# The first norm's sums of a hybrid decoder layer, placed later inside the first projection

## The chip, the cores and the metric

The kernel runs on one core of a Trainium2 chip. The metric is device microseconds of one execution; where several executions were timed, the median counts. The engines are named as in the profile: PE multiplies matrices (PEld loads its weights), DVE and ACT work on vectors, POOL is GpSimd, SP issues DMAs.

## The reference

One layer works on a sequence of 1024 positions and 1024 channels:

```
z = rms_norm(x, norm_mix_g);  proj = z @ w_in
u_pool, u_lru, u_gate = proj[:512], proj[512:1024], proj[1024:]
y_pool = pool_mixer(u_pool)                   # trailing windows 2, 4, 8, 16
y_lru  = rg_lru(conv(u_lru)) * gelu(u_gate)   # 4 taps, sigmoid gates, a scan
h = x + concat(y_pool, y_lru) @ w_out
h = h + square(relu(rms_norm(h) @ w_up)) @ w_down
h = h + sigmoid(rms_norm(h) @ w_gate + b) * (p @ w_proj)
out = rms_norm(h)
```

Here `rms_norm(x, g)` is `x * rsqrt(mean(x*x) + eps) * g`, with the mean over the 1024 channels of a position.

## The kernel before, in words

Channels lie on the 128 partitions and positions along the free dimension, so `x` is eight blocks `H[k]` of 128 channels by 1024 positions. Every fp32 product is made of three: an operand is split by ACT into a rounded part `hi` (L178, or L181 with the gain as a scale) and by DVE into the rest `lo` (L179, L182), and PE multiplies hi·hi, hi·lo and lo·hi (`mm`, L350). A `mm` over 1024 positions is six matmuls of 128x512.

**The first norm.** The factor rsqrt(mean) of a position isn't needed before the projection: the product is made of `x * g`, and its result is multiplied by the factor afterwards (`normed`, L535). The factor needs the sum of the squares over all channels. ACT squares each block (L386, L389), DVE adds the squares up in `T[0]` (L390); then `norm.sums()` splits that sum into hi and lo for each half of 512 positions (DVE: L414, L415; the tiles are called `hl`) and multiplies it by a matrix of ones on PE (L416, L417: four matmuls into two banks called `n_ps`, two for each half), which sums over the partitions and leaves the sum in all of them. `norm.rstd(R)` calls `sums` and goes on from the banks: DVE transposes each (L434), ACT takes the root of 16 columns for each half (L438, which first needs another activation table, ACT_TABLE_LOAD), DVE inverts it (L439) and spreads it back into `R` (L440).

**The first projection.** The three first outputs `ps_l0`, `ps_l1`, `ps_l2` (the first three blocks of `u_lru`) are built up together, since the blocks of `x` arrive one by one: for each block `k`, `mm` for `o` = 0, 1, 2, 18 matmuls in all. From `k` = 2 on that is the loop at the end of the function's part shown below. In the last block, `k` = 7, `norm.rstd(R)` is called ahead of this loop, so that its four matmuls stand on PE's queue between block 6 and block 7. The other nine outputs, `ps_i0` to `ps_i8`, follow one by one (`project`, 48 matmuls each, weights `wi0` to `wi8`).

**What follows on the other engines.** `conv(0..2)` take `ps_l0` to `ps_l2` through `normed`, a scale on ACT (L540) and three taps on DVE (L544), and split the result (`y8` to `y11` and `y20` to `y23`, hi and lo in turn). `ask_small` splits the small weights of the gates and the pool mixer, `T[5]`, into `hl` as well: ACT writes its hi (L178, `hl<-t`), DVE its lo (L179, `hl<-t,hl`). They are the same tiles `hl` that hold the hi and lo of the norm's sums, so ACT's copy can start only when the sums of the first half have been multiplied. Then come the pool windows (L621 to L631), the gates of the recurrence (`lru_gates`: `ps_g`, L571 on PE, two banks for each of two row halves; sigmoids L579 on ACT; a product L582 on DVE) and the scan (`lru_scan`: L591 to L602).

**PSUM.** Outputs take turns (`psum`): one pair of banks from `pp` (`banks`), the next two single banks from `pd` (`bank`), of which there are four. The norm's sums take two of `pd`. A name such as `ps_i4_0` is the first bank of an output in two single banks. The output `ps_g03` (gate 3, first row half) takes the two banks in which `ps_i4` was, so its matmuls wait until `normed` on DVE (L535) has read `ps_i4` out of them.

**What sets the order.** The program's layer orders the instructions of each engine by priorities that follow the order of the Python code; instructions that are "pinned" (`pin`, `keep_in_program_order`) stay where they are written. On a core each engine works its list in order; semaphores join the lists. The norm's matmuls are not pinned at this place.

Of the kernel before, what the change touches and what calls it, by code (L numbers as in the profile page):

```python
# [30 lines left out]
NT = D // P  # L31
# [27 lines left out]
def block_kernel(  # L59
# [22 lines left out]
    def fixed(name, dt):  # L82
        return pool.tile([P, S], dt, name=name)
# [27 lines left out]
    R = fixed("rstd", F32)  # L111
# [34 lines left out]
    def f32(ap):  # L146
        return ap.bitcast(F32)
# [3 lines left out]
    def turns(z):  # L151
        return z.rearrange("p (a j) -> p j a", a=2)
# [11 lines left out]
    def col(name, i):  # L164
        c = COLS[name] + i
        return vecs[:, c : c + 1]
# [3 lines left out]
    def pin(ins):  # L170
        return tc.keep_in_program_order(ins) if in_order else ins
# [3 lines left out]
    def split(src, hi, lo, g=None, eng=None):  # L175

        if g is None:
            first = pin(nc.scalar.activation(hi, src, AF.Copy))  # L178
            lowest[:] = [pin((eng or nc.vector).tensor_tensor(lo, src, f32(hi), ALU.subtract)).ins]  # L179
        else:  # L180
            first = pin(nc.scalar.activation(hi, src, AF.Identity, scale=g))  # L181
            lowest[:] = [pin(nc.vector.scalar_tensor_tensor(lo, src, g, f32(hi), ALU.mult, ALU.subtract)).ins]  # L182
        return first.ins

    def raw_tile(name):
        return wp.tile([P, S], F32, tag="raw", name=f"{name}_raw")

    def weight_tiles(name):
        return [wp.tile([P, S], F32R, tag=f"w{x}", name=f"{name}_{x}") for x in ("hi", "lo")]
# [141 lines left out]
    def ask():  # L331
        if todo:
            fn, *args = todo.pop()
            asked.append(fn(*args))

    def weights():
        ask()
        return asked.pop(0)

    def mm(parts, whi, wlo, zhi, zlo, first, last, only=None, more=False, held=False):  # L340
        outs = [
            (slice(hs.start + n, hs.start + min(n + HALF, w)), ps[:, n : min(n + HALF, w)])
            for hs, ps in parts
            for w in (hs.stop - hs.start,)
            for n in range(0, w, HALF)
            if only is None or hs.start + n == only.start
        ]
        for w, z in ((whi, zhi), (whi, zlo), (wlo, zhi)):
            for hs, ps in outs:
                ins = nc.tensor.matmul(  # L350
                    ps, w, turns(z[:, hs]),
                    start=first and z is zhi and w is whi,
                    stop=last and w is wlo,
                    skip_group_check=more,
                )
                if held:
                    tc.keep_in_program_order(ins)
                    held = False

    def kblk(t, k):  # L360
        return t[:, k * P : (k + 1) * P]
# [80 lines left out]
    def tables():  # L442

        one = ones_f[:, :16]
        tc.keep_in_program_order(
            nc.vector.tensor_tensor_scan(recip_t, one, one, 0.0, ALU.mult, ALU.add)
        )
        nc.vector.reciprocal(recip_t, recip_t)


        nc.sync.dma_start(T[5][:, FIRST], gates)
        nc.sync.dma_start(T[5][:, SECOND], pool_w)
# [5 lines left out]
    def softplus():  # L458

        c0 = COLS["lru_l"]  # L460
        lv = vecs[:, c0 : c0 + NLRU]
        with tc.issue_after(lowest[0]):
            nc.vector.tensor_scalar_mul(neg, lv, -1.0)
        nc.vector.tensor_tensor(e, lv, neg, ALU.max)
        nc.scalar.activation(e, e, AF.Exp, scale=-1.0)
        nc.vector.tensor_scalar_add(s, e, 2.0)
        nc.vector.reciprocal(s, s)
        nc.vector.tensor_tensor(s, s, e, ALU.mult)
        nc.vector.tensor_tensor(s2, s, s, ALU.mult)
        nc.vector.memset(poly, 1.0 / 19)  # L470
        for n in range(8, -1, -1):
            nc.vector.tensor_tensor(poly, poly, s2, ALU.mult)
            nc.vector.tensor_scalar_add(poly, poly, 1.0 / (2 * n + 1))
        nc.vector.tensor_tensor(poly, poly, s, ALU.mult)
        nc.vector.tensor_scalar(neg, neg, 0.0, 8.0, ALU.max, ALU.mult)
        nc.vector.scalar_tensor_tensor(cpos, poly, 16.0, neg, ALU.mult, ALU.add)
        nc.vector.tensor_scalar_mul(cneg, cpos, -1.0)

        c_b, c_s = COLS["pool_b"], COLS["pool_s"]
        with tc.issue_after(lowest[0]):  # L480
            nc.vector.tensor_tensor(pool_bs, vecs[:, c_b : c_b + NPOOL], vecs[:, c_s : c_s + NPOOL], ALU.mult)

    norm = Norm("n0", T[0], T[1:3])
# [4 lines left out]
    for k in range(NT):  # L488
        halves = HALVES if k < 2 else (slice(0, S),)
        if k == 1:  # L490
            whi, wlo = weights()
        for hs in halves:
            nc.sync.dma_start(H[k][:, hs], xT[k * P : (k + 1) * P, hs])
            if k == hs.start == 0:
                raw = raw_tile("wl0")[:, : 3 * P]
                whi, wlo = (t[:, : 3 * P] for t in weight_tiles("wl0"))
                nc.sync.dma_start(raw, w_lru[:P, :])
                pin(nc.vector.tensor_copy(whi, raw))
            split(H[k][:, hs], A[k][0][:, hs], A[k][1][:, hs], col("g_mix", k))
            if k > 1:  # L500
                whi, wlo = weights()
            if k == hs.start == 0:
                pin(nc.vector.tensor_tensor(wlo, raw, f32(whi), ALU.subtract))
        for i in AFTER[k] if k < len(AFTER) else (k,):
            norm.add(H[i])
        if k == NT - 1:
            in_order.clear()
            ask()
        if k == 2:
            softplus()  # L510
        if k == 3:
            tables()
        if k == NT - 1:
            norm.rstd(R)
        if k < 2:

            for hs in HALVES:
                for o in range(3):
                    mm(ps_l[o], kblk(whi, o), kblk(wlo, o), *A[k], k == 0, False, hs)
            continue  # L520
        for o in range(3):
            mm(ps_l[o], kblk(whi, o), kblk(wlo, o), *A[k], False, k == NT - 1)


# [157 lines left out]
    norm = Norm("n1", T[4], T[5:])  # L682
# [550 lines left out]
```

## Time and profile before

| what | value |
|---|---|
| median of 3 runs | 927.12 us |
| lowest and highest of them | 926.88 and 928.76 us |
| the profiled execution, its own time | 927.23 us |
| its span, first to last instruction | 925.4 us |
| granted TensorE clock in the span | 0.998 |
| instructions | 11180 |

The profiled execution took 1.8 us more than its span, and 0.11 us more than the median. A row of the timeline gives start and duration in us, engine, line, operation, the tile written `<-` the tiles read (without their numbers), the size and the count; in brackets stands how long the engine had been idle before it, and whose result ended that. Consecutive like instructions are merged into a row, whose duration then goes from the first start to the last end. Matmuls overlap: a 128x512 matmul shows as 0.38 us, but the next can start 0.22 us after it.

### The profile page before, as it was taken

The page shows a single profiled execution, that of the slowest core. Times are in us where ns is not written, and L with a number is a line of the kernel's source. Part 1 is how long each engine was busy: PE and PEld are TensorE (multiplying, and loading weights), DVE is VectorE, ACT ScalarE, POOL GpSimd, SP SyncE. Part 2 cuts the span into 40 slices and gives each one's busy share as a digit, 9 for nine tenths or more (in the row PEclk, how much of TensorE's full clock was granted, in tenths as well). Part 3 has the DMA queues.
Part 4 walks back from the last instruction along what each step waited for, and adds up shares of the span by engine and source line. Part 5 has one row for each costly group of instructions (what it writes and reads, how often), then busy time and mean ns, then how long its engine had stood idle before and what let it go on. Part 6 is the DMA issues. An engine that isn't in the chain of part 4 may idle for free.

```text
span 925.4 us, 11180 instructions
## 1 busy us (share of the span) xinstructions
PE 915.3 (99%) x4351; PEld 798.5 (86%) x4351; DVE 758.8 (82%) x903; ACT 456.5 (49%) x531; POOL 5.6 (1%) x7
## 2 busy tenths in 40 slices
PE   9999999999999999999999999999999999999996
PEld 7888888888888888888888888888888888888895
DVE  7997985659998888888888989979776679885676
ACT  7567893447543343344334654443444347652544
POOL 0000000002000000000000000000000000000000
PEclk9999999999999999999999999999999999999999
DMA  7210143211244345344534989366532341031022
GB/s 265 99 47 23 46 151 122 69 45 54 84 175 178 125 161 197 142 138 173 191 125 148 341 317 342 110 202 208 188 111 92 118 156 45 16 122 46 1 91 91
DMA packets 45044, 123.97 MB, mean 134 GB/s; under 512 B 4160, under 2 KB 6208, under 8 KB 44992
## 3 DMA queue, kind: packets, MB, share of 16 engines
q1 hardware_dynamic: 44848, 123.22, 38.3%
q8 instruction: 34, 0.56, 0.3%
q14 instruction: 18, 0.15, 0.0%
q10 hardware_dynamic: 144, 0.04, 0.0%
HBM read 89.69 MB, written 33.55 MB: 133 GB/s over the span
## 4 chain that ended last, share of the span: by engine, by line
PE 95%; DVE 2%; issue 1%; DMA 1%; SPq 0%; ACT 0%; DVEq 0%
PE ps_P_d L350 31%; PE ps_P_u L350 31%; PE ps_i L350 10%; PE ps_e L350 10%; PE ps_o L350 9%; PE ps_j L350 1%; DMA h<-in_xT 1%; PE ps_g L571 1%; PE ps_p L350 1%; DVE t L390 1%; PE ps_l L350 0%; DVE wl_lo L179 0%; PE n_ps L417 0%; DVE t L1093 0%; DVE a L182 0%
## 5 line engine op out<-in xcount | busy, mean ns | idle before, releaser
L350 PE MATMUL ps_P_d<-a,wd_P_hi 128*128 128x512 f32 x880 | 261.7, 379 | 0.0
L350 PEld LDWEIGHTS ps_P_d<-a,wd_P_hi 128*128 128x128 f32 x880 | 166.3, 189 | 23.6
L350 PE MATMUL ps_P_d<-a,wd_P_lo 128*128 128x512 f32 x440 | 166.8, 379 | 0.0
L350 PE MATMUL ps_P_u<-a,wu_hi 128*128 128x512 f32 x512 | 152.3, 379 | 0.0
L350 PE MATMUL ps_P_u<-y,wu_hi 128*128 128x512 f32 x384 | 114.2, 379 | 0.0
L350 PEld LDWEIGHTS ps_P_u<-a,wu_hi 128*128 128x128 f32 x512 | 96.8, 189 | 13.8
L350 PE MATMUL ps_P_u<-a,wu_lo 128*128 128x512 f32 x256 | 97.0, 379 | 0.0
L350 PEld LDWEIGHTS ps_P_d<-a,wd_P_lo 128*128 128x128 f32 x440 | 83.2, 189 | 11.8
L350 PEld LDWEIGHTS ps_P_u<-y,wu_hi 128*128 128x128 f32 x384 | 72.6, 189 | 10.4
L747 DVE TENSOR_TENSOR t<-t,ps_P_u 128x512 f32<-128x512 f32 (+1 forms) x80 | 62.6, 782 | 20.4 <-PE ps_P_u L350 20.4
L350 PE MATMUL ps_i<-a,wi_hi 128*128 128x512 f32 x288 | 74.3, 380 | 0.0
L350 PE MATMUL ps_P_u<-y,wu_lo 128*128 128x512 f32 x192 | 72.8, 379 | 0.0
L178 ACT ACTIVATE a<-wd 128x1024 fp32r<-128x1024 f32 x56 | 58.9, 1054 | 21.4 <-PE ps_P_d L350 11.6
L179 DVE TENSOR_TENSOR a<-wd,a 128x1024 fp32r<-128x1024 f32 x56 | 67.2, 1221 | 1.0 <-ACT a L178 0.6
L350 PE MATMUL ps_o<-y,wo_hi 128*128 128x512 f32 x256 | 65.7, 379 | 0.0
L350 PEld LDWEIGHTS ps_i<-a,wi_hi 128*128 128x128 f32 x288 | 54.1, 189 | 8.8 <-issue 1.0
L178 ACT ACTIVATE wu_hi<-wu 128x1024 fp32r<-128x1024 f32 x24 | 25.4, 1057 | 69.8 <-PE ps_P_u L350 44.2
L178 ACT ACTIVATE wu_hi<-wu_raw 128x1024 fp32r<-128x1024 f32 (+1 forms) x26 | 25.2, 974 | 66.3 <-PE ps_P_u L350 41.3
L350 PEld LDWEIGHTS ps_o<-y,wo_hi 128*128 128x128 f32 x256 | 48.4, 189 | 6.8
L350 PEld LDWEIGHTS ps_P_u<-a,wu_lo 128*128 128x128 f32 x256 | 48.4, 189 | 6.8
L178 ACT ACTIVATE wd_P_hi<-wd 128x1024 fp32r<-128x1024 f32 x24 | 25.3, 1054 | 46.9 <-PE ps_P_d L350 46.8
L389 ACT ACTIVATE t<-h 128x512 f32<-128x512 f32 (+2 forms) x44 | 32.0, 731 | 28.3 <-DVE h L1052 20.5
(223 smaller groups left out, 1502.8 us busy)
## 6 DMA issues: line engine op xcount, KB each, us to landing
wd<-act SPq DMA_DIRECT2D x56, 512.0 KB, 5.7
act<-t SPq DMA_DIRECT2D x32, 512.0 KB, 4.3
wu_raw<-in_w_up SPq DMA_DIRECT2D x16, 512.0 KB, 3.4
wu<-in_w_up SPq DMA_DIRECT2D x16, 512.0 KB, 3.9
act<-wu SPq DMA_DIRECT2D x16, 512.0 KB, 4.6
wd<-in_w_down SPq DMA_DIRECT2D x16, 512.0 KB, 6.2
h<-in_xT SPq DMA_DIRECT2D x14, 512.0 KB, 4.4
wg_raw<-in_w_gate SPq DMA_DIRECT2D x10, 512.0 KB, 3.2
```

The source lines that it names most:

```text
L178: first = pin(nc.scalar.activation(hi, src, AF.Copy))
L179: lowest[:] = [pin((eng or nc.vector).tensor_tensor(lo, src, f32(hi), ALU.subtract)).ins]
L350: ins = nc.tensor.matmul(ps, w, turns(z[:, hs]), start=first and z is zhi and w is whi, stop=last and w is wlo, skip_group_check=more,)
L389: pin(nc.scalar.activation(sq, t[:, hs], AF.Square))
L390: self.eng.tensor_tensor(self.acc[:, hs], self.acc[:, hs], sq, ALU.add)
L571: nc.tensor.matmul(x, w[r, o * P : (o + 1) * P], turns(z[r, at : at + HALF]), start=n == 0, stop=n == 2)
L747: (eng or nc.vector).tensor_tensor(to, to if y is None else y, x, ALU.add)
```

## The change

In the last block of the loop `norm.rstd(R)` is called between the second and the third output, instead of ahead of the first:

```diff
         if k == 3:
             tables()
-        if k == NT - 1:
-            norm.rstd(R)
         if k < 2:
 
             for hs in HALVES:
@@ -519,6 +517,8 @@
                     mm(ps_l[o], kblk(whi, o), kblk(wlo, o), *A[k], k == 0, False, hs)
             continue
         for o in range(3):
+            if k == NT - 1 and o == 2:
+                norm.rstd(R)
             mm(ps_l[o], kblk(whi, o), kblk(wlo, o), *A[k], False, k == NT - 1)
```

No instruction is added or removed: each engine has as many rows as before, and the lists of POOL and SP are the same. On PE the four matmuls move. This is PE's list around the end of block 7's second output (`ps_l1`, two single banks), with + where the norm's matmuls now stand; they stood, in the same order, ahead of the first matmul of `ps_l0` with `wl7`, 12 matmuls earlier.

```order
@@ -106,4 +102,8 @@
 L350 MATMUL ps_l1_0_148<-a_70,wl7_lo_408 128x512
 L350 MATMUL ps_l1_512_149<-a_70,wl7_lo_408 128x512
+L416 MATMUL n0_ps0_432<-hl0_135,ones_142 128x512
+L417 MATMUL n0_ps0_432<-hl0_135,ones_142 128x512
+L416 MATMUL n0_ps512_437<-hl1_136,ones_142 128x512
+L417 MATMUL n0_ps512_437<-hl1_136,ones_142 128x512
 L350 MATMUL ps_l2_150<-a_70,wl7_hi_407 128x512 x4
 L350 MATMUL ps_l2_150<-a_70,wl7_lo_408 128x512 x2
```

So the norm's sums come behind `ps_l0` and `ps_l1` of the last block and ahead of its `ps_l2`. The split of the sums on DVE (L414, L415) stays in its place; behind it DVE's lo of `wi0` (L179) now comes ahead of both transposes, where it stood between them.

The order that the priorities give changes in a few places further on. On DVE this is the piece around the first pool window (L621 to L631; `t_68` are the pool's tiles, `y23` the lo of the fourth convolution, `y1` that of the first pool window, L582 the product of the first gate):

```order
 L621 TENSOR_TENSOR t_68<-t_68 128x1023
 L622 COPY t_68<-t_68 128x1
-L631 SCALAR_TENSOR_TENSOR t_68<-t_68 128x1023
 L179 TENSOR_TENSOR y23_131<-h_67,y22_130 128x1024
 L629 TENSOR_TENSOR t_68<-t_68,recip_t_69 128x1
+L631 SCALAR_TENSOR_TENSOR t_68<-t_68 128x1023
+L630 TENSOR_TENSOR t_68<-t_68 128x1
 L582 TENSOR_TENSOR h_67<-h_67 128x1024
-L630 TENSOR_TENSOR t_68<-t_68 128x1
 L179 TENSOR_TENSOR y1_114<-t_68,y0_113 128x1024
```

L630, the last step of the pool window, now stands ahead of L582 instead of behind it, and L631 behind `y23` instead of ahead of it.

On ACT this is the piece around `y2`, the hi of the second pool window, and the last sigmoids of the second gate, ahead of the table load for the first scan's exponentials (L591):

```order
 L579 ACTIVATE t_68<-ps_g11_512_696,vecs_137 64x512
 L579 ACTIVATE h_67<-ps_g01_694,vecs_137 64x1024
+L579 ACTIVATE h_67<-ps_g11_0_695,vecs_137 64x512
 L178 ACTIVATE y2_115<-t_68 128x1024
-L579 ACTIVATE h_67<-ps_g11_0_695,vecs_137 64x512
 L579 ACTIVATE h_67<-ps_g11_512_696,vecs_137 64x512
 L591 ACT_TABLE_LOAD
```

One of the two sigmoids that stood between `y2` and the table load now stands ahead of `y2`. In the same way, further up on ACT's list, the hi of `wi2` comes ahead of that of `y8`, the hi of `wi3` ahead of `y20`, and a sigmoid of `ps_g10` ahead of `y22`.

## Prediction

> **What bounds the kernel now.** I read the page first: busy times, then the chain that ended last.
>
> ```profile
> PE 915.3 (99%) x4351; PEld 798.5 (86%) x4351; DVE 758.8 (82%) x903; ACT 456.5 (49%) x531; POOL 5.6 (1%) x7
> PE 95%; DVE 2%; issue 1%; DMA 1%; SPq 0%; ACT 0%; DVEq 0%
> ```
>
> PE is busy for all but 10.1 us of 925.4, and 95% of the chain that ended last lies on it. So time comes out only where PE waits. The view of PE's waits names all of them, and the chain in order of time shows what follows.
>
> ```profile
> PE n_ps L416 <- DVE hl L414: 0.6, 1, 0.6
> PE n_ps L417 <- DVE hl L415: 0.4, 1, 0.4
> PE n_ps L426 <- DVE t L1153: 0.4, 1, 0.4
> PE n_ps L426 <- ACT t L1146: 0.3, 1, 0.3
> ...
> 39.72 20.72 PE ps_i L350 x96
> ...
> 909.46 5.37 PE ps_e L350 x48
> ```
>
> The view has one more, of 1.1 us at the start. Two of the rows shown lie at the very end; the first two are those of the moved matmuls, on the split of the sums by DVE. From 35.84 to 914.8 us the chain then stays on PE without a gap. So what PE gains before 40 us reaches the end, **unless PE meets a result later that doesn't come earlier with it**. That is the question of this prediction.
>
> **Term 1: PE around block 7.** The timeline of PE and of DVE:
>
> ```profile
> 32.66 0.59 PE L350 MATMUL ps_l<-a,wl_lo 128*128 128x512 f32 x2
> 33.80 0.49 PE L416 MATMUL n_ps<-hl,ones 128*128 128x512 f32 x1 [0.55 <-DVE hl L414]
> 35.68 1.02 PE L350 MATMUL ps_l<-a,wl_hi 128*128 128x512 f32 x4
> 39.56 1.03 PE L350 MATMUL ps_i<-a,wi_hi 128*128 128x512 f32 x4
> ...
> 34.00 1.29 DVE L415 TENSOR_TENSOR hl<-t,hl 128x512 fp32r<-128x512 f32 x2
> ```
>
> The chain gives 20.72 / 96 = 0.216 us for a matmul. Block 6's last one starts at 32.66 + 0.22 = 32.87, so block 7 could start at 33.09; it starts at 35.68. In the change its first two outputs stand there: 12 x 0.216 = 2.59, to 35.68. Then come the sums. Their last operand is there at 34.00 + 1.29 = 35.29, 0.39 us before PE asks for the first, so the wait goes whole. Four sums without a wait stand later in the same trace:
>
> ```profile
> 250.93 0.40 PE L416 MATMUL n_ps<-hl,ones 128*128 128x512 f32 x1
> ...
> 251.86 0.59 PE L350 MATMUL ps_P_u<-y,wu_hi 128*128 128x512 f32 x2
> ```
>
> They take 251.86 - 250.93 = 0.93. Then `ps_l2`, 6 x 0.216 = 1.30: `ps_i0` starts at 35.68 + 0.93 + 1.30 = 37.91 instead of 39.56, **1.65 us earlier**. That is the most that the change can give; no other wait of PE is left to take away. Block 7's own operands are split ahead of the sums on DVE's list and are no limit.
>
> **Term 2: the chain of the factor.** ACT and DVE get the sums later. The timelines of ACT and DVE:
>
> ```profile
> 35.27 1.06 ACT L178 ACTIVATE hl<-t 128x1024 fp32r<-128x1024 f32 x1 [1.36 <-PE n_ps L417]
> 36.35 1.28 ACT L438 ACT_TABLE_LOAD   x1
> 37.65 0.53 ACT L438 ACTIVATE edge<-rstd,eps 128x16 f32<-128x16 f32 x2
> ...
> 37.02 0.71 DVE L434 STREAM_TRANSPOSE rstd<-n_ps 128x512 f32<-128x512 f32 x1
> 37.65 1.18 DVE L179 TENSOR_TENSOR hl<-t,hl 128x1024 fp32r<-128x1024 f32 x1
> 38.75 0.35 DVE L439 RECIPROCAL edge<-edge 128x16 f32<-128x16 f32 x2
> 40.26 0.65 DVE L535 TENSOR_TENSOR t<-ps_l,rstd 128x512 f32<-128x512 f32 x1
> ```
>
> ACT's copy into `hl` waits for the first half's sums. They now end at 35.68 + 0.23 + 0.40 = 36.31, so the copy starts at 36.35, 1.08 us later; the table load and the roots stand behind it on ACT, to 38.73 and 39.26. Before, the roots were done at 38.18 and the inverse waited until 38.75 because DVE was in its `hl` row; so 0.57 of the 1.08 was covered. Now the second inverse starts at about 39.29 instead of 38.91: **DVE's stream of convolutions starts 0.38 us later**, at 40.64. DVE's two transposes are no limit: they start at 36.35 and end some 1.4 us later, at about 37.75, before `ps_i0`'s second matmul takes the second bank at 37.91 + 0.22.
>
> What the table load costs is a place for the skill. The Trainium skill ("ScalarE: Activation LUTs", section "What ACT_TABLE_LOAD costs") gives 1283 ns for the load and a drain of about 1380 ns with it. The 1.28 agrees with the first; the drain isn't in this trace, since the roots start 0.02 us after the load's end. By the page's sum this chain would be 1.38 us longer, and of the gain worked out below about 0.3 would be left. I go by the rows, and keep the other case as rival 4.
>
> **Term 3: where the two meet.** PE is 1.65 us early and DVE 0.38 late, so each place where PE waits for DVE loses 2.03 us of slack. In the timeline the tightest is `ps_g03`, whose banks DVE must empty of `ps_i4` (L535, two halves):
>
> ```profile
> 108.12 1.28 DVE L535 TENSOR_TENSOR t<-ps_i,rstd 128x512 f32<-128x512 f32 x2
> 109.47 0.92 PE L571 MATMUL ps_g<-y,hl 64*128 64x512 f32 x6
> ```
>
> The second half is free at 109.40. The six matmuls run in pairs, (0.92 - 0.38) / 2 = 0.27 apart, and the second pair, at about 109.74, writes it. From DVE's end to PE's start pass 0.04 to 0.05 us, as the chain shows at the moved wait:
>
> ```profile
> 34.08 0.61 DVE hl L415
> 34.70 0.04 issue
> 34.74 0.50 PE n_ps L417
> ```
>
> So PE's net gain at `ps_g03` is the smaller of 1.65 and 109.74 - 109.40 - 0.05 - d = 0.29 - d, where d is DVE's shift at this place. **With d = +0.38 nothing is left.** Elsewhere there is room. DVE's lo of `wi2`, for instance, is done at 59.14 and first used by PE at 62.83:
>
> ```profile
> 57.92 1.22 DVE L179 TENSOR_TENSOR wi_lo<-wi_raw,wi_hi 128x1024 fp32r<-128x1024 f32 x1
> 62.83 0.59 PE L350 MATMUL ps_i<-a,wi_lo 128*128 128x512 f32 x2
> ```
>
> From 145 us on DVE's work starts from PE's outputs and moves with them.
>
> So d has to be followed. Two reorderings shorten DVE's and ACT's lists.
>
> ```profile
> 68.58 1.22 DVE L631 SCALAR_TENSOR_TENSOR t<-t 128x1023 f32<-128x1023 f32 x1
> 69.72 1.22 DVE L179 TENSOR_TENSOR y<-h,y 128x1024 fp32r<-128x1024 f32 x1
> 70.92 1.22 DVE L582 TENSOR_TENSOR h<-h 128x1024 f32<-128x1024 f32 x1
> 72.06 0.15 DVE L630 TENSOR_TENSOR t<-t 128x1 f32<-128x1 f32 x1
> 73.33 1.23 DVE L179 TENSOR_TENSOR y<-t,y 128x1024 fp32r<-128x1024 f32 x1 [1.12 <-ACT y L178]
> ```
>
> Before, DVE ends the pool window with L630 and then idles 1.12 us while ACT copies it. Now L630 comes ahead of L582, which fills that time. From 68.58 + 0.38 = 68.96: `y23` and L629 1.20 (69.72 to 70.92), L631 1.14 (68.58 to 69.72), L630 0.15, ACT's copy 1.06 and 0.06 of handing over. `y1` starts at 72.57 instead of 73.33: d = -0.76. Likewise on ACT:
>
> ```profile
> 80.71 1.06 ACT L178 ACTIVATE y<-t 128x1024 fp32r<-128x1024 f32 x1 [2.81 <-DVE t L630]
> 81.79 1.25 ACT L579 ACTIVATE h<-ps_g,vecs 64x512 f32<-64x512 f32 x2
> 83.06 1.28 ACT L591 ACT_TABLE_LOAD   x1
> 88.57 1.23 DVE L595 SCALAR_TENSOR_TENSOR h<-h 128x1024 f32<-128x1024 f32 x1 [4.26 <-ACT h L593]
> ```
>
> One of the two sigmoids behind `y2` moves into the 2.81 us that ACT idled ahead of it: the table load comes another (83.06 - 81.79) / 2 = 0.6 earlier, and DVE at 88.57 waits for what follows that load, so d = -1.36. From there to 109.4 DVE's rows follow each other without idle time, and d stays. The gain is the smaller of 1.65 and 0.29 + 1.36 = 1.65: the banks are just free in time. I take **1.6**, allowing a few hundredths for that wait.
>
> No DMA is issued by the moved step, and SP's list is unchanged; DVE's lo of `wi0` frees its raw buffer 0.7 us earlier, the later ones move with d, and those blocks are multiplied some 10 us after they land.
>
> Sum: 927.23 - 1.6 = 925.63 for the profiled execution; the median of the runs shown is 0.11 lower, so 927.12 - 1.6 = **925.5 us**, 0.17% less. I call a change within 0.2% (1.85 us, about what a measurement of this kernel can tell from none) the same.
>
> **The rivals.**
> 1. *The gain is given back at `ps_g03`.* If the reorderings save nothing, d = +0.38, PE waits there for the rest, and the time is 927.1 to 927.2. If only the first works, d = -0.76, 1.05 is kept: 926.1. For it: the slack was 0.29, and the places of two or three rows decide. Against: both idle times stand in the trace, with work that is ready for them.
> 2. *DVE blocks behind `y23`* and the kernel is slower. `y23` now stands ahead of L631 and waits for ACT's `y22`, which now stands behind one sigmoid more, the second row here:
>
> ```profile
> 63.76 3.65 ACT L579 ACTIVATE h<-ps_g,vecs 64x512 f32<-64x512 f32 x5
> 68.59 1.11 ACT L579 ACTIVATE h<-ps_g,vecs 64x1024 f32<-64x1024 f32 x1
> ```
>
> If ACT starts its sigmoids no earlier than at 63.76, `y22` comes 1.1 us later and DVE idles ahead of `y23`; with the filled gap lost as well d = 0.38 + 1.1 = 1.5. PE would then be 1.2 us later at `ps_g03` than before: 928.3. It decides from d = +0.29 on; past 0.2% only from d = 2.1. Against it: `wi3`'s hi, ahead of `y20` now, is made while ACT idles for `y20`'s operand, so the sigmoids start some 0.6 earlier.
> 3. *More than PE's waits show*: no row gives over 1.65, so this is the spread of runs alone (926.88 is 0.24 below the median): 925.2 or a little less.
> 4. *The roots start later behind the table load* than 0.02 us, now that DVE's `hl` row no longer hides it. With as much again as the load itself (1.28), d = -0.08, 0.37 is kept: 926.75. Against: in the trace of before the roots start right at the load's end, 36.35 + 1.28 against 37.65. This is what the drain on the page named under term 2 would look like.
>
> **How the numbers follow.** Forecast, gain 1.3 to 1.65 (925.4 to 925.9): 0.55. Rival 1: 0.22. Rival 2: 0.10. Rival 3: 0.10. Rival 4: 0.03. Faster by over 0.2% means below 925.27: rival 3 and, since the forecast lies 0.25 us from that bound and runs differ by as much, a third of its 0.55: 0.28. Slower by over 0.2% (above 928.97): most of rival 2 stays short of it, and one of the three runs before stood at 928.76: 0.06. The same: 0.66. The range goes from 925.0 (1.65 and half a microsecond of spread) to 927.3 (all given back); outside lie most of rival 2 and a little of rival 3.
>
> **What would show it.** PE without a wait at L416 and L417, and `ps_i0` at 37.9; ACT's `hl` copy at 36.35 and roots at 38.7; `normed` at 40.6; no idle time ahead of `y1`, at 72.6; the table load of L591 at 81.7; `ps_g03` at 107.8 with at most 0.2 of waiting. A wait of PE on L535 of over 0.5 there would make rival 1 right, idle time of DVE ahead of `y23` rival 2. Wrong altogether would be a new wait of PE after 145 us.

## The result and the profile after

The changed kernel takes **926.08 us** (median of 21 runs, 925.45 to 927.16), the kernel before in the same comparison 927.32 us (median of 21, 926.88 to 928.89). The ratio is 0.9984, with a 95% interval of 0.9978 to 0.9991: 1.24 us less, 0.13%, on the side that was forecast and within the 0.2% that I called the same. The forecast was 925.5, a gain of 1.6. The interval leaves the gain anywhere from 0.8 to 2.0 us, so the medians alone can't tell 1.24 from 1.6. The question is whether the traces show where the other 0.36 us went.

The span of the profiled execution fell from 925.4 to 924.5 us, by 0.9. This is PE's view of waits after (us in total, times, longest):

```profile
PE ps_l L487 <- DVE heat L367: 1.1, 1, 1.1
PE ps_l L350 <- ACT a L181: 0.5, 1, 0.5
...
PE ps_l L350 <- DVE a L182: 0.3, 1, 0.3
```

The two rows of L416 and L417 that were to go are gone. Two others are new, both in the first blocks, and they stand in the chain that ended last:

```profile
1.65 5.23 DMA h<-in_xT
6.91 0.73 ACT a L181
7.66 0.76 DVE a L182
8.47 27.89 PE ps_l L350 x128
...
37.30 1.29 PE ps_l L350 x6
```

The chain no longer goes through DVE's split of the sums. It goes back to the landing (the end of the load) of the second half of the first block of x at 6.88 us, and from 8.47 to 913.9 us it is PE without a gap. The timeline of PE after, at the sums and at `ps_g03`:

```profile
33.61 1.03 PE L350 MATMUL ps_l<-a,wl_hi 128*128 128x512 f32 x4
...
36.20 0.40 PE L416 MATMUL n_ps<-hl,ones 128*128 128x512 f32 x1
...
37.14 1.03 PE L350 MATMUL ps_l<-a,wl_hi 128*128 128x512 f32 x4
...
38.43 0.81 PE L350 MATMUL ps_i<-a,wi_hi 128*128 128x512 f32 x3
...
108.35 1.76 PE L571 MATMUL ps_g<-y,hl 64*128 64x512 f32 x12
110.03 1.13 PE L350 MATMUL ps_i<-a,wi_hi 128*128 128x512 f32 x4
```

The sums take 37.14 - 36.20 = 0.94 us with no wait, and `ps_i0` starts 38.43 - 33.61 = 4.82 us after block 7, which is the prediction's 37.91 - 33.09 to the hundredth. But block 7 starts at 33.61 here and not at 33.09. And the row of `ps_g03` takes 1.76 us, where in the kernel before it took 1.56:

```profile
109.47 1.56 PE L571 MATMUL ps_g<-y,hl 64*128 64x512 f32 x12
110.97 1.13 PE L350 MATMUL ps_i<-a,wi_hi 128*128 128x512 f32 x4
```

So this pair of executions adds up as 1.65 (the stall), less 0.52 (block 7 later), less 0.20 (inside `ps_g03`), 0.93 in all: 110.97 - 110.03 = 0.94 behind that place, and 0.9 in the spans. ACT and DVE after:

```profile
36.87 1.06 ACT L178 ACTIVATE hl<-t 128x1024 fp32r<-128x1024 f32 x1 [2.43 <-PE n_ps L417]
37.94 1.28 ACT L438 ACT_TABLE_LOAD   x1
39.24 0.53 ACT L438 ACTIVATE edge<-rstd,eps 128x16 f32<-128x16 f32 x2
```

```profile
69.57 1.23 DVE L179 TENSOR_TENSOR y<-h,y 128x1024 fp32r<-128x1024 f32 x1 [0.18 <-ACT y L178]
...
73.20 1.23 DVE L179 TENSOR_TENSOR y<-t,y 128x1024 fp32r<-128x1024 f32 x1
...
107.42 1.28 DVE L535 TENSOR_TENSOR t<-ps_i,rstd 128x512 f32<-128x512 f32 x2
```

The roots start 0.02 us after the load's end, DVE waits 0.18 us ahead of `y23`, and `y1` (73.20) has no idle time ahead of it.

### The profile page after: what moved, and what is told of

Its sections match the earlier page's. It is cut to its first block, busy times and chain, and to the rows that moved or that the text cites. A ratio compares the mean times of both kernels' runs of the same rounds, so it can differ in the third digit from the quotient of the medians.

```text
span 924.5 us, 11179 instructions
## 1 busy us (share of the span) xinstructions
PE 914.5 (99%) x4351; PEld 797.8 (86%) x4351; DVE 758.6 (82%) x903; ACT 456.4 (49%) x531; POOL 5.8 (1%) x7
## 4 chain that ended last, share of the span: by engine, by line
PE 98%; DVE 1%; DMA 1%; ACT 0%; SPq 0%; DVEq 0%; issue 0%
PE ps_P_d L350 31%; PE ps_P_u L350 31%; PE ps_i L350 10%; PE ps_e L350 10%; PE ps_o L350 9%; PE ps_l L350 3%; PE ps_j L350 1%; PE ps_g L571 1%; DMA h<-in_xT 1%; PE ps_p L350 1%; DVE t L1093 0%; PE n_ps L417 0%; PE n_ps L416 0%; DVE a L182 0%; ACT a L181 0%; PE n_ps L426 0%
## 5 line engine op out<-in xcount | busy, mean ns | idle before, releaser
L179 DVE TENSOR_TENSOR a<-wd,a 128x1024 fp32r<-128x1024 f32 x56 | 67.2, 1220 | 1.0 <-ACT a L178 0.6
```

## The experiments

After the first profile two theories stood. **A**: the gain is PE's stall, less a late start of the first blocks (which the stall used to hide and now nothing hides), less the short wait at `ps_g03`. **B**: the start plays no part, and the difference to the forecast is the spread of runs, or is lost elsewhere. In each comparison below the kernel before ran too: 927.16 us (33 runs, e1 to e4), 927.22 (33, e5 to e8), 927.33 (27, e9 to e11); the others have 11 runs each.

**e1, the changed kernel again**, no edit.

> The changed kernel once more, unaltered. Theory A: the gain is the 1.65 us that PE no longer waits, less what the old stall used to hide of a late start (0.52 us in the profiled execution), less PE's wait for the banks of ps_g03 (0.2). A execution that starts like that of before (second row of L181 at 6.1) then has block 7 at 33.1 and a span 1.4 to 1.5 us shorter than before; one that starts late again (6.9) has 33.6 and about 0.9. In both ps_g03 shows a wait of 0.1 to 0.3. Median 925.8 to 926.2. Rival B: the start plays no part, the shortfall of 0.4 us is spread of runs; span and start don't go together. Rival C: the shortfall lies later than 145 us, and a new wait of PE shows there.

925.93 us (925.39 to 926.58), ratio 0.9985 (0.9976 to 0.9994), span 923.9. Its execution has an early landing. ACT's row of the second half, then PE's and DVE's timelines:

```profile
6.10 0.72 ACT L181 ACTIVATE a<-h,vecs 128x512 fp32r<-128x512 f32 x1 [1.59 <-DMA h<-in_xT]
```

```profile
32.99 1.03 PE L350 MATMUL ps_l<-a,wl_hi 128*128 128x512 f32 x4
...
37.82 1.03 PE L350 MATMUL ps_i<-a,wi_hi 128*128 128x512 f32 x4
...
107.73 1.75 PE L571 MATMUL ps_g<-y,hl 64*128 64x512 f32 x12
109.42 1.13 PE L350 MATMUL ps_i<-a,wi_hi 128*128 128x512 f32 x4
```

```profile
33.31 0.76 DVE L414 CAST hl<-t 128x512 fp32r<-128x512 f32 x2
...
72.59 1.23 DVE L179 TENSOR_TENSOR y<-t,y 128x1024 fp32r<-128x1024 f32 x1
...
106.81 1.28 DVE L535 TENSOR_TENSOR t<-ps_i,rstd 128x512 f32<-128x512 f32 x2
```

With DVE's cast at 33.31 (33.32 in the profile of before) this is the fair pair. `ps_i0` is 39.56 - 37.82 = 1.74 earlier, and behind `ps_g03` 110.97 - 109.42 = 1.55 are left; the span is 1.5 shorter. No wait of PE later than this is new, so rival C falls. The same kernel gave 924.5 with the landing at 6.91 and 923.9 with it at 6.10, and block 7 moved by 0.62, the span by 0.6.

**e2, the sums after the first output.**

```diff
-            if k == NT - 1 and o == 2:
+            if k == NT - 1 and o == 1:
                 norm.rstd(R)
```

> The sums stand between the first and second output of block 7, six matmuls earlier. Their last operand comes 0.2 to 0.3 us after PE asks, so PE waits about 0.25 there and ps_i0 starts about 1.4 us earlier than before. But in DVE's list L582 now stands ahead of y23, so nothing is left to fill the 1.1 us ahead of y1, and on ACT both sigmoids stand behind y2 again: DVE reads ps_i4 at about the time of before (shift d about 0). Theory A (the gain is the smaller of what PE gains at the sums and 0.29 - d at ps_g03): PE waits about 1.1 us at ps_g03, and 0.3 us is left: 927.0 (926.7 to 927.2). Rival B (what PE no longer waits at the sums is the gain): 925.9, 0.2 above the changed kernel at most.

926.76 us, ratio 0.9996 (0.9987 to 1.0005). PE's timeline and DVE's row of `ps_i4`:

```profile
33.17 1.03 PE L350 MATMUL ps_l<-a,wl_hi 128*128 128x512 f32 x4
...
38.45 1.03 PE L350 MATMUL ps_i<-a,wi_hi 128*128 128x512 f32 x4
...
108.81 1.85 PE L571 MATMUL ps_g<-y,hl 64*128 64x512 f32 x12 [0.38 <-DVE t L535]
110.60 1.13 PE L350 MATMUL ps_i<-a,wi_hi 128*128 128x512 f32 x4
```

```profile
107.98 1.28 DVE L535 TENSOR_TENSOR t<-ps_i,rstd 128x512 f32<-128x512 f32 x2
```

PE gained 39.56 - 38.45 = 1.11 at the sums and kept 110.97 - 110.60 = 0.37. DVE's shift is d = 107.98 - 108.12 = -0.14, and the formula of the prediction, 0.29 - d, gives 0.43. Theory A: **two thirds of the gain were given back at one pair of banks**. (The wait at the sums was 38.45 - 33.17 - 4.82 = 0.46, more than the 0.25 that I expected, since PE was early and DVE's split 0.2 late in this execution.)

**e3, the sums after the third output.**

```diff
         for o in range(3):
-            if k == NT - 1 and o == 2:
-                norm.rstd(R)
             mm(ps_l[o], kblk(whi, o), kblk(wlo, o), *A[k], False, k == NT - 1)
+            if k == NT - 1 and o == 2:
+                norm.rstd(R)
```

> The sums stand behind the third output, just ahead of ps_i0: no wait for their operands, but DVE's transposes of them then end about 1 us after ps_i0 wants its second bank, and ACT's copy into hl starts at 37.65, 1.3 us later than in the changed kernel. Theory A: PE waits 0.7 to 1.0 at ps_i0, of 1.65 some 0.7 is left there; DVE's convolutions start 1.3 us later (normed at about 41.9), but its list fills the time ahead of y1 and the table load of L591 stands ahead of y2, so ps_g03 takes away little: 926.4 (926.1 to 926.9). Rival B (only the waits at L416 and L417 count): 925.6 to 926.0, as the changed kernel.

926.36 us, ratio 0.9991 (0.9982 to 1.0). The wait comes at the place named, the first row of `ps_i0`:

```profile
39.35 0.67 PE L350 MATMUL ps_i<-a,wi_hi 128*128 128x512 f32 x2 [0.43 <-DVE rstd L434]
```

Block 7 starts at 33.92 in this execution, so `ps_i0` comes 39.35 - 33.92 - 4.82 = 0.61 later than without waits; the row of `ps_g03` is 1.56, without a wait. e1's median, with this wait more and that of 0.19 inside `ps_g03` less, gives 925.93 + 0.61 - 0.19 = 926.35. The size of the wait was 0.1 under the lower end expected; the sum fits.

**e4, DVE reads `ps_i4` two places earlier**, in the changed kernel.

```diff
     ps = project(4)
     lru_gates(2)
-    normed(T[0], ps)
+    with tc.high_priority(URGENT): normed(T[0], ps)
```

> The changed kernel, with DVE's reading of ps_i4 (L535) two places earlier in its list, so that the banks of ps_g03 are free over 2 us earlier; the lists of PE and ACT are the same. Theory A: the wait of 0.2 us inside ps_g03 goes (its row is 1.5 to 1.6 again instead of 1.76) and the time falls by 0.1 to 0.2 against the changed kernel: 925.9 if that has 926.1. Rival B (the wait there costs nothing, or PE meets the same limit at the next place): the same time as the changed kernel, within 0.05; slower if y4's lo, now one or two places later, is late for PE.

926.09 us, ratio 0.9987 (0.9978 to 0.9996). PE's timeline:

```profile
38.50 1.03 PE L350 MATMUL ps_i<-a,wi_hi 128*128 128x512 f32 x4
...
108.42 1.56 PE L571 MATMUL ps_g<-y,hl 64*128 64x512 f32 x12
109.91 1.13 PE L350 MATMUL ps_i<-a,wi_hi 128*128 128x512 f32 x4
```

From `ps_i0` to the matmul behind `ps_g03` pass 109.91 - 38.50 = 71.41 us, against 109.42 - 37.82 = 71.60 in e1 and the same in the first profile after: the wait is gone and 0.19 us with it, to the end (span less `ps_i0`: 885.9 against 886.1). The medians don't show it: 926.09 against 925.93. The landing was at 6.98 in this profile, and a start that moves by 0.6 hides 0.19 in eleven runs. The trace bears theory A out; the time neither way.

**e5 and e6, a later start of PE**, in the kernel before and in the changed one.

```diff
-WARM = 9
+WARM = 16
```

> The kernel before with 16 instead of 9 warming matmuls ahead of the first projection, so that PE starts the projection 7 x 0.39 us later. 36 matmuls of 0.216 us follow up to 14 us, and PE idled 1.3 us among them for its operands, so block 7 comes 1.3 to 1.5 us later than in the profile of before, at about 34.5. Theory A: the stall at the sums (1.65 us, set by DVE's split, which doesn't wait for PE) hides that: block 7 starts at 35.6 to 35.8 as before, the waits at L416 and L417 are nearly gone, and the time is that of before, within 0.2 us. Rival B (a late start is paid whatever stands at the sums): 1.3 us more, 928.5.

> The changed kernel with the same 16 warming matmuls. Theory A: there is no stall left to hide the late start, so the whole of it reaches the end: block 7 at about 34.4, ps_i0 at 39.2, and the time 1.1 to 1.4 us above the changed kernel (its own late landings, 0 to 0.6 us, are covered by the later start): 927.0 to 927.4, nothing left of the gain. Rival B (late start paid by both alike, the gain is a constant 1.2 us): the difference to the kernel before with 16 warming matmuls stays 1.2 us.

e5: 928.26 us, ratio to the kernel before 1.0013 (1.0004 to 1.0022). e6: 926.9 us, 0.9997 (0.9988 to 1.0006). The difference is 1.36, as theory B said, and the 1.0 that e5 costs was not in theory A's number. The traces say why. DVE's and PE's timelines of e5:

```profile
34.16 0.77 DVE L414 CAST hl<-t 128x512 fp32r<-128x512 f32 x2
```

```profile
34.64 0.49 PE L416 MATMUL n_ps<-hl,ones 128*128 128x512 f32 x1
...
36.52 1.03 PE L350 MATMUL ps_l<-a,wl_hi 128*128 128x512 f32 x4
...
40.40 0.81 PE L350 MATMUL ps_i<-a,wi_hi 128*128 128x512 f32 x3
```

With more warming matmuls the program's layer also put DVE's small rows of a softplus series (L472, L473, 128x4 elements each) in other places. In e5 several stand back to back and start 0.2 us apart (16.22, 16.41, 16.62); in the profile of before a long row often follows such a row, and starts 0.07 us behind it (22.66, 22.73). DVE's cast is 34.16 - 33.32 = 0.84 later. PE came to the sums 34.64 - 33.25 = 1.39 later than before, but block 7 only 36.52 - 35.68 = 0.84 later: PE's own lateness was hidden, DVE's was not. So the mechanism is A's, and my expectation had missed that the edit moves DVE too. In the profiled execution of e6, one of its faster ones (926.48 us), the 16 matmuls took 5.4 us instead of 6.2 (last section), block 7 started at 33.81 and `ps_i0` at 38.63, again 4.82 later, though DVE's cast stood at 34.12. As a test on times the pair failed; e9 and e10 take its place.

**e7 and e8, an earlier start**, in the kernel before and in the changed one: the first weights on ACT's queue.

```diff
-                nc.sync.dma_start(raw, w_lru[:P, :])
+                nc.scalar.dma_start(raw, w_lru[:P, :])
```

> The kernel before, with the load of the first weights issued by ACT's queue instead of SP's, so that the second half of the first x block and all loads behind it are issued 0.45 us earlier on SP; the lists of the engines are otherwise those of before but for four small rows of the softplus. PE should start block 7 about 0.4 us earlier (32.7). Theory A: the stall at the sums takes it up, since DVE's split sets its end: 927.1, within 0.2 of before. Rival B: 0.4 us less, 926.7.

> The changed kernel, with the same load on ACT's queue. Theory A: the earlier start reaches the end, since nothing at the sums takes it up any more (their last operand is there at about 35.1, and PE asks at about 35.2): 0.3 to 0.5 us less than the changed kernel, 925.5, and runs lie closer together because the late landings of the second half (rows of L181 at 6.9 to 7.2) come 0.45 us earlier. Rival B: no difference to the changed kernel, 926.0.

e7: 927.7 us; its runs lie in two groups, four at 926.42 to 926.72 and six at 927.62 to 928.63, and one of 2515.59 stands apart; ratio 1.0 (0.9991 to 1.0009). e8: 926.07, 0.9989 (0.9981 to 0.9998). The edit didn't do what it was for. DVE's rows of the first weights' cast, e7 and then e8 (4.10 in the profile of before):

```profile
5.36 0.36 DVE L498 CAST wl_hi<-wl_raw 128x384 fp32r<-128x384 f32 x1 [3.96 <-DMA wl_raw<-in_w_lru]
...
33.70 0.76 DVE L414 CAST hl<-t 128x512 fp32r<-128x512 f32 x2
```

```profile
5.16 0.36 DVE L498 CAST wl_hi<-wl_raw 128x384 fp32r<-128x384 f32 x1 [3.76 <-DMA wl_raw<-in_w_lru]
```

The weights landed over 1 us later and PE began later and not earlier. As readings the two still count. In e7 PE came to the sums at 34.93, 1.7 us later than before, and `ps_i0` at 39.94, 0.38 later: as much as DVE's cast (33.70 against 33.32). In e8 block 7 started at 33.31 and `ps_i0` at 38.13.

**e9 and e10, DVE's split earlier**, in the kernel before and in the changed one. Six of the nine terms of the softplus series are left out.

```diff
-        nc.vector.memset(poly, 1.0 / 19)
-        for n in range(8, -1, -1):
+        nc.vector.memset(poly, 1.0 / 7)
+        for n in range(2, -1, -1):
```

> The kernel before with 12 of the 18 small rows of the softplus series left out on DVE (6 of its 9 terms; the value changes by less than 2e-5 of itself), so that DVE reaches the split of the sums earlier; PE's, ACT's and SP's lists are the same. Such a row takes 0.07 to 0.2 us of DVE's list in the trace of before, 0.9 to 1.2 us in all. Theory A (in the kernel before ps_i0 starts 6.24 us after DVE's first cast L414, whenever PE gets to the sums; so in three profiles so far): L414 at 32.2 to 32.6, ps_i0 at 38.4 to 38.8, 926.2 to 926.5. Rival B (what is lost at the sums is PE's, by its place in the program): 927.2.

> The changed kernel with the same 12 rows left out (the same change of the value). Theory A (in the changed kernel ps_i0 starts 4.82 us after PE begins block 7, whatever DVE does; so in five profiles so far): DVE's split comes about 1 us earlier and nothing follows from it; the time of the changed kernel, 926.0, within 0.2. Together with e9 the gain of the change shrinks from 1.2 to 0.2 to 0.5 us. Rival B: as before the change, the gain stays 1.2.

e9: 926.44 us, ratio to the kernel before 0.9992 (0.9983 to 1.0001). e10: 925.92, 0.9986 (0.9977 to 0.9994). The twelve small rows on DVE bring the kernel before 0.9 us and the changed kernel nothing that its spread lets see (925.92 against 925.93 in e1), so that the gain of the change shrinks from 1.2 to 0.52, where theory A had 0.2 to 0.5. The interval of e9's ratio just reaches 1.0, but ten of its eleven runs lie below 926.65, the fastest of the 27 of the kernel before beside it. DVE and PE in e9:

```profile
32.62 0.76 DVE L414 CAST hl<-t 128x512 fp32r<-128x512 f32 x2
```

```profile
33.61 0.40 PE L416 MATMUL n_ps<-hl,ones 128*128 128x512 f32 x1
...
38.86 1.03 PE L350 MATMUL ps_i<-a,wi_hi 128*128 128x512 f32 x4
```

This execution has a late landing (L181's row at 6.91), as the first profile after: PE comes to the sums at 33.61 instead of 33.25. It doesn't matter, `ps_i0` stands 38.86 - 32.62 = 6.24 behind DVE's cast. In e10 the cast stands at 32.53, 0.8 earlier than in e1, and `ps_i0` comes 38.20 - 33.39 = 4.81 behind block 7.

The spread of the runs says the same as these traces. If a late start is hidden by the stall and paid without it, the changed kernel must spread more. The middle half of all 114 runs of the kernel before lies within 0.5 us, that of the 32 runs of the changed kernel (e1's among them) within 0.7; for e9 it is 0.2 and for e10 0.7.

**e11, e2 and e4 together**: sums after the first output, `ps_i4` read earlier (both edits above).

> The sums between the first and second output, as in e2, and DVE's reading of ps_i4 two places earlier, as in e4. Theory A: what e2 lost was PE's wait at ps_g03 for that reading (0.38 ahead of the row and 0.3 inside it): both go, the row is 1.5 to 1.6 again and 0.6 us come back: 926.1 to 926.2, as the changed kernel. Rival B (e2 lost by its wait at the sums, 0.25, and by its later orders): it stays at 926.7.

926.2 us, ratio 0.9988 (0.9980 to 0.9997), against 926.76 in e2. The row of `ps_g03`:

```profile
108.50 1.56 PE L571 MATMUL ps_g<-y,hl 64*128 64x512 f32 x12
```

The wait is gone and 0.56 us are back. From `ps_i0` to the matmul behind `ps_g03` pass 109.99 - 38.59 = 71.40 us, against 110.60 - 38.45 = 72.15 in e2: what e2 had lost was the wait for those banks. The landing was late here (7.05, block 7 at 33.76), so PE didn't wait at the sums either.

The ten profiles with the sums where the kernel before or the changed kernel has them (e2, e3 and e11 have them elsewhere), with DVE's cast L414, the time at which PE has done what stands ahead of the sums (kernels with the sums first) or starts block 7 (sums inside it), and the start of `ps_i0`:

| kernel | L414 | PE | `ps_i0` | `ps_i0` less L414 | `ps_i0` less PE |
|---|---|---|---|---|---|
| before | 33.32 | 33.25 | 39.56 | 6.24 | 6.31 |
| e5 | 34.16 | 34.64 | 40.40 | 6.24 | 5.76 |
| e7 | 33.70 | 34.93 | 39.94 | 6.24 | 5.01 |
| e9 | 32.62 | 33.61 | 38.86 | 6.24 | 5.25 |
| after | 33.10 | 33.61 | 38.43 | 5.33 | 4.82 |
| e1 | 33.31 | 32.99 | 37.82 | 4.51 | 4.83 |
| e4 | 33.19 | 33.68 | 38.50 | 5.31 | 4.82 |
| e6 | 34.12 | 33.81 | 38.63 | 4.51 | 4.82 |
| e8 | 32.61 | 33.31 | 38.13 | 5.52 | 4.82 |
| e10 | 32.53 | 33.39 | 38.20 | 5.67 | 4.81 |

With the sums first, `ps_i0` follows DVE's cast, though PE comes to the sums 0.07 us ahead of it in one profile and 1.23 behind it in another. With the sums inside block 7 it follows PE, though the cast lies anywhere from 0.86 ahead of block 7's start to 0.32 behind it. That is the change in two constants. The first can hold only within a limit that no profile here reaches: PE's own part is 4.82 us, so a PE that came more than 6.24 - 4.82 = 1.42 us behind the cast would set `ps_i0` itself.

## Why the prediction was right, and what it lacked

- **Term 1, PE around block 7: right.** The stall goes whole; 4.82 from block 7 to `ps_i0`, as worked out, in six profiles.
- **The sum failed in one step: that block 7 starts at 33.09.** I took this from one execution, whose stall had no part in it, and set it as if it were fixed. In the seven profiles whose sums stand inside block 7 or right behind it and whose start-up is unchanged (after, e1, e2, e3, e4, e10, e11) it is 33.61, 32.99, 33.17, 33.92, 33.68, 33.39 and 33.76, with ACT's row of x's second half at 6.91, 6.10, 6.32, 7.22, 6.98, 6.69 and 7.05. In the five from 6.69 on block 7 starts 26.70 to 26.71 after that row; in the two earlier ones (26.89 and 26.85) PE doesn't wait for it. Before, none of this reached the end (e9); now all of it does. Their mean is 33.50, 0.41 later than mine; 1.65 - 0.41 - 0.19 = 1.05, against a measured 1.24. (The other end of the difference was typical: DVE's cast stood at 33.32 before, and at 33.10 to 33.51, with a mean of 33.31, in after, e1 to e4 and e11, whose DVE lists are the same up to it.) For the size of that mean seven profiles are few; that a late start is hidden before and paid after is shown by e9, e5 and e7 against e1 and the first profile after.
- **Term 2, the chain of the factor: right.** For block 7 at 33.09 I had the `hl` copy at 36.35, the roots at 38.73 and the first `normed` at 40.64; e1, with block 7 at 32.99, has 36.26, 38.63 and 40.53. For the drain of the Trainium skill's page "ScalarE: Activation LUTs" (section "What ACT_TABLE_LOAD costs") there is no room after either: the roots start 0.02 us behind the load.
- **Term 3, the meeting at `ps_g03`: right, a little small.** `y1` at 72.57 was forecast, 72.59 is in e1; d = -1.36 was forecast, 106.81 - 108.12 = -1.31 came. The first of these is partly luck: ahead of `y23` DVE was 0.17 earlier than forecast and then waited 0.18 for ACT's `y22`, which the forecast had at nothing. I allowed 0.05 for the wait inside `ps_g03`; it is 0.19. That wait doesn't depend on the start, since DVE's stream now begins at PE's sums and moves with them: in the first profile after, block 7 is 0.62 later than in e1, d is 107.42 - 108.12 = -0.70, and the row takes 1.76 where that of e1 takes 1.75. In e1, with the cast as before, the gain is 1.55 behind that place, against the forecast of 1.6.
- **Rival 1** took 0.19 and not 1.65. It was no idle fear: with other places of two or three rows (e2) it took 0.74. **Rival 2**: ACT's later `y22` made DVE wait 0.18, not 1.1. **Rival 3**: nothing beyond the waits, 1.55 at most. **Rival 4**: not seen.

What stays open: why the second half of x comes at times 0.6 to 1.1 us later than in the profile of before (6.13). The one edit aimed at it (e7, e8) moved another landing instead. And e5's and e9's medians moved by 0.2 more than their `ps_i0` (1.04 against 0.84, 0.9 against 0.70), which is within the spread of eleven runs and wasn't followed. The profiled execution of e10, the slowest of its eleven, loses a further 0.4 us between 503 and 534 us, where the chain that ended last leaves PE; no other profile shows that, and its span (924.7) is not compared here.

No version beats the changed kernel by more than runs differ. e4 takes a further 0.19 us off in the trace.

## What to carry to other kernels

A wait is the difference of two arrivals, and it hides whatever makes the waiting engine late. Taking it away is worth the wait in one trace less the mean of what it hid, so look at how far the waiting engine's arrival moves from execution to execution, not only at the wait. Ask also which list sets the other arrival: here leaving out twelve small rows on DVE gave 0.9 us in the medians, and 0.7 in the trace, without moving a matmul. And a move on the bounding engine reorders the lists of the others: the same move, six matmuls earlier, lost two thirds of its gain at one pair of banks 70 us later, and got it back when one reading moved up by two places.

## What the runs showed of the hardware

- The first matmuls run at half pace for a time that differs between executions. By their weight loads, the 16 warming matmuls of e5 run 0.43 us apart to 7.00 us; those of e6 run 0.43 apart to 5.30 and then 0.22 apart. The granted clock reads 1.00 in both (columns here: the slice and its length, PE busy, weight loads busy, granted clock, DMA share, GB/s; e5, then e6):

```profile
5.00:6.00 1.00, 1.00 (x4) 0.32 (x3) 1.00 0.72 192
```

```profile
5.00:6.00 1.00, 1.00 (x6) 0.37 (x5) 1.00 0.86 232
```

- The same load of 256 KB, issued at 1.65 us in each, let ACT start between 6.10 and 7.22 us in the profiles of the same start-up.
- Issuing the first weights from a second queue at nearly the same time let DVE start on them 1.1 to 1.3 us later (e7, e8), with both halves of x issued beside them.
